# Modulation products of a two-stream transformer: one two-row accumulation, or four 32-column strips of the array

## The chip, the cores and the metric

The kernel runs on one core of a Trainium2 chip (trn2). The metric is device time in microseconds (us) of one execution; a kernel's figure is the median of its runs. A profiled execution leaves a trace of every instruction, with its engine (PE is TensorE's matmuls, PEld its weight loads, DVE VectorE, ACT ScalarE, POOL GpSimd, SP SyncE) and what it waited for.

## The reference

Two residual streams of 256 tokens by 1024 channels (`x` and a context stream) go through two blocks and a last block of another kind, all in float32. Each of the first two blocks normalizes, mixes (a recurrent branch with 16 heads, a convolution branch, a gate), normalizes again and runs a lookup over 16384 experts. Both norms and both residual additions are modulated. The modulation depends on one conditioning vector for each stream:

```python
# silu of the conditioning vector, times a [1024, 6144] matrix, plus a bias
mod = silu(c) @ p['ada_w'] + p['ada_b']
shift1, scale1, gate1, shift2, scale2, gate2 = split(mod, 6)
h = rmsnorm(x, g) * (1 + scale1) + shift1
```

For one layer that is two vectors of 1024 times 48 output tiles of 128 columns; for both layers 96 tiles, whose weights take 512 KB each. Only two columns, one for each stream, are ever multiplied with these weights.

## The kernel before, in words

Channels lie on the 128 partitions, a vector of 1024 as 8 pieces (k tiles), tokens on the free axis (512, both streams side by side). Weights are read as float32 tiles of [128, 8, 128]; `wtile` (L227) loads one on SP's queue, ACT rounds it into `whi` (L238) and DVE writes the rest into `wlo` (L240). `lin` (L251) multiplies with three products for each k tile (`whi` with the high and the low half of the activation, `wlo` with the high half), so a 128 x 512 output (`zps`, `gtps`, `zaps`, `zbps`) takes 24 matmuls at L258.

The **modulation** is made in units of two output tiles by `ada` (L271). Each unit loads two weight tiles `adaw` (SP, L277), multiplies the 8 k tiles of each into two rows of a PSUM tile `adaps` (L279: the stationary operand is `cs`, two columns; the 128 weight columns stream past), copies the two rows to `adarow` (ACT, L281), turns each 2 x 128 piece over with a transpose (L283) and adds the bias into `mod` (DVE, L284). There are 48 units. Eight, with scale 1 and shift 1 of layer 0, stand at the start of the first mixer, ahead of `modnorm` (L326), which forms `ngm` (L335) and then for each k tile `nt` (DVE, L342), `h` (ACT, L344) and the low half of `h` (DVE, L345). 24 are dealt into the mixer of layer 0 and 16 into that of layer 1, the letters 'A' of the table `PLAN` (L33). These share the tag "wraw" with the weights of `wtile`, two buffers, and so also their order on SP's queue.

A **mixer** goes through eight pairs of heads. A pair has a projection and decay part (`ssps` L417, `wps`, `aps` L437, with gate products `gtps`), a score part (`scps` L485, `sc` DVE L489, the turning `btps` L499) and a chain of chunk steps that wait for one another (`bp` L571, `up` L580, `zp` L585, `yp` L557). Other work is put between the parts at places that `PLAN` names; `pop` (L287) starts it, with priorities moved by `BUMP` (L35). What then stands where on each engine is settled by a list scheduler from priorities and estimated durations. So a change in the products changes the order of other work too. ACT reloads its function table (ACT_TABLE_LOAD) where one kind of function follows another.

After the mixer of layer 0 comes its expert lookup, then mixer and lookup of layer 1, then the last block; in the lookups and the last block no unit stands.

`self.blk` (L189) is a constant with two blocks of 64 x 64 ones, the stationary operand of `ssps`.

Of the kernel before, what the change touches and what calls it, by code (L numbers as in the profile page):

```python
# [11 lines left out]
F32 = mybir.dt.float32  # L12
# [4 lines left out]
AF = mybir.ActivationFunctionType  # L17
ALU = mybir.AluOpType
# [4 lines left out]
P = 128  # L23
D = 1024
KO = 8
# [152 lines left out]
class Core:  # L178
# [3 lines left out]
    def consts(self):  # L182
        nc, tc = self.nc, self.tc
        cp = self.cp = self.ctx.enter_context(tc.tile_pool(name="const", bufs=1, reuse_waits="tile"))
        self.ident = cp.tile([P, P], F32, name="ident")
        make_identity(nc, self.ident)
        self.onesd = cp.tile([P, P], F32, name="onesd")
        nc.vector.memset(self.onesd, 1.0 / D)
        self.blk = cp.tile([P, P], F32, name="blk")  # L189
        nc.vector.memset(self.blk, 0.0)  # L190
        nc.vector.memset(self.blk[0:64, 0:64], 1.0)
        nc.vector.memset(self.blk[64:128, 64:128], 1.0)
        self.rmask = cp.tile([P, 2, P], F32, name="rmask")
        nc.scalar.dma_start(self.rmask, self.A["rmask"])
        self.reset = cp.tile([P, 8 * 65], BF16, name="reset")
        nc.vector.memset(self.reset, 1.0)
        nc.vector.memset(self.reset[:, ::65], 0.0)
        self.iota = cp.tile([P, P], F32, name="iota")
        nc.scalar.dma_start(self.iota, self.A["iota"])
        self.cb = {}  # L200
        for n, v in (("neps", NORM_EPS), ("lneps", 4 * LN_EPS), ("gneps", GN_EPS), ("ln512", math.log(512.0)), ("one", 1.0)):
            self.cbias(n, v)
        self.pv = []
        for l in range(2):
            t = cp.tile([P, NPV], F32, name=f"pv{l}")
            nc.scalar.dma_start(t, self.A["pv"][l])
            self.pv.append(t)
        self.pv2 = cp.tile([P, NPV2], F32, name="pv2")
        nc.scalar.dma_start(self.pv2, self.A["pv2"])
        self.mod = [cp.tile([P, 48, 2], F32, name=f"mod{l}") for l in range(2)]  # L210
# [49 lines left out]

    def silu_c(self):
        nc, tc = self.nc, self.tc
        self.cs = self.cp.tile([P, KO, 2], F32, name="cs")
        with tc.tile_pool(name="adap", bufs=1, reuse_waits="tile") as ap:
            c = ap.tile([P, KO, 2], F32, name="cT")
            nc.scalar.dma_start(c, self.A["cT"])
            nc.scalar.activation(self.cs, c, AF.Tanh, scale=0.5)
            nc.vector.tensor_scalar(self.cs, self.cs, 0.5, 0.5, op0=ALU.mult, op1=ALU.add)
            nc.vector.tensor_mul(self.cs, self.cs, c)

    def ada(self, l, m0, n, wpool, wtag, bufs, pp, tag):  # L271

        nc = self.nc
        ps = pp.tile([P, 512], F32, tag=tag, name="adaps")
        for i in range(n):
            w = wpool.tile([P, KO, P], F32, tag=wtag, name="adaw", bufs=bufs)
            nc.sync.dma_start(w, self.A["ada"][l, m0 + i])  # L277
            for k in range(KO):
                nc.tensor.matmul(ps[0:2, i * P:i * P + P], self.cs[:, k, :], w[:, k, :], start=k == 0, stop=k == KO - 1)  # L279
        row = self.wp.tile([2, 2 * P], F32, tag="adarow", name="adarow", bufs=1)  # L280
        nc.scalar.copy(row[:, :n * P], ps[0:2, :n * P])  # L281
        for i in range(n):
            nc.tensor.transpose(ps[:, 2 * i:2 * i + 2], row[:, i * P:i * P + P], self.ident[0:2, 0:2])  # L283
        nc.vector.tensor_tensor(self.mod[l][:, m0:m0 + n, :], ps[:, 0:2 * n].rearrange("p (m c) -> p m c", c=2),  # L284
                                self.par(l, "ada_b", m0, n).unsqueeze(2).to_broadcast([P, n, 2]), op=ALU.add)

    def pop(self, where):  # L287
# [1476 lines left out]
```

## Time and profile before

| | us |
|---|---|
| median of 3 runs (lowest, highest) | 5218.21 (5210.64, 5221.29) |
| profiled execution, by its own time | 5211.48 |
| span of the trace in it | 5209.7 |
| PE busy | 4967.9 (95%) |
| PE weight loads busy | 4170.8 (80%) |
| DVE busy | 3488.0 (67%) |
| ACT busy | 2561.0 (49%) |
| POOL busy | 182.2 (3%) |

Busy times overlap, since the engines run side by side. Matmuls are pipelined, and the end of one is modelled, so that a busy TensorE is not one at its peak. The mean granted clock of TensorE over the span is 0.965 of full speed. "Waits" name the instruction or transfer whose end released the waiting one; the chain is followed back from the last instruction, each time to what released it. A matmul of float32 operands leaves two records in the trace (two passes), so the 768 products of the modulation are 1536 records. Rows show the form of a matmul as stationary rows * columns, then the moving tile.

### The profile page before, as it was taken

Reading aid. Unit: us, or ns where it says so; the run is one execution under the profiler, and the core shown is the slowest. Engines: PE = TensorE matmul, PEld = TensorE weight load, DVE = VectorE, ACT = ScalarE, POOL = GpSimd, SP = SyncE. Lnnn points to the kernel's source line nnn. Section 1 sums busy time; section 2 is a strip of 40 time slices with the busy share of each in tenths; the row PEclk is TensorE's granted clock in tenths of the full one; section 3 lists DMA queues with packets and bytes.
Section 4 is the critical chain, followed back from the end, with each engine's and each line's share of the span. In section 5 each row is a group of like instructions: output and inputs, shape, how many; then the busy total and the mean of one; then the engine's idle time right before and its main releaser. Section 6 shows DMA issues by size and latency. Waiting matters only on the chain.

```text
span 5209.7 us, 86462 instructions
## 1 busy us (share of the span) xinstructions
PE 4967.9 (95%) x33298; PEld 4170.8 (80%) x33298; DVE 3488.0 (67%) x7830; ACT 2561.0 (49%) x4754; POOL 182.2 (3%) x409
## 2 busy tenths in 40 slices
PE   8999998999999999999999999998899999989989
PEld 6677776678777888888887787877889999987888
DVE  4888878558995455555555566656796777765654
ACT  4345444534989322222223445445478544455564
POOL 0000001000000000000000010101000000000000
PEclk9999999999999999999999899888999999999999
DMA  4332323543444644444442332323656877733544
GB/s 137 107 91 88 90 81 93 167 151 101 160 171 163 234 144 142 142 143 142 143 146 70 111 84 78 85 61 92 210 187 222 279 227 238 226 116 118 167 131 146
DMA packets 432974, 740.50 MB, mean 142 GB/s; under 512 B 132210, under 2 KB 273202, under 8 KB 427826
## 3 DMA queue, kind: packets, MB, share of 16 engines
q1 hardware_dynamic: 431042, 732.29, 44.1%
q8 instruction: 262, 4.29, 0.3%
q10 hardware_dynamic: 1520, 2.69, 0.1%
q14 instruction: 150, 1.23, 0.1%
HBM read 622.37 MB, written 112.49 MB: 141 GB/s over the span
## 4 chain that ended last, share of the span: by engine, by line
PE 74%; ACT 12%; DVE 8%; DMA 3%; issue 2%; SPq 0%; ACTq 0%; POOL 0%; DVEq 0%; POOLq 0%
PE v L1180 20%; PE s L258 14%; PE zps L258 5%; ACT ws L1126 3%; PE adaps L279 3%; PE qps L258 2%; PE ops L258 2%; PE gtps L258 2%; ACT pt L1121 2%; PE ops L1368 2%; ACT whi L238 2%; ACT pt L1120 2%; PE bp L571 1%; DVE wlo L240 1%; PE zbps L258 1%
## 5 line engine op out<-in xcount | busy, mean ns | idle before, releaser
L258 PE MATMUL s<-h,whi 128*128 128x512 f32 (+1 forms) x4096 | 1058.7, 343 | 1.3 <-ACT whi L238 0.7
L240 DVE TENSOR_TENSOR wlo<-wraw,whi 128x1024 fp32r<-128x1024 f32 (+2 forms) x602 | 724.7, 1205 | 470.9 <-ACT whi L238 458.4
L238 ACT CAST whi<-wraw 128x1024 fp32r<-128x1024 f32 (+2 forms) x602 | 621.9, 1034 | 727.0 <-PE s L258 200.0
L258 PEld LDWEIGHTS s<-h,whi 128*128 128x128 f32 x4096 | 703.8, 191 | 68.6 <-ACT ge L1136 1.0
L258 PE MATMUL s<-h,wlo 128*128 128x512 f32 (+1 forms) x2048 | 704.2, 344 | 9.1 <-DVE wlo L240 9.1
L1180 PE MATMUL v<-al,vh 128*128 128x512 f32 (+1 forms) x2048 | 689.7, 337 | 0.6 <-DVE al L953 0.6
L1180 PE MATMUL v<-ah,vl 128*128 128x512 f32 (+1 forms) x2048 | 689.2, 337 | 0.0
L1180 PE MATMUL v<-ah,vh 128*128 128x512 f32 (+1 forms) x2048 | 682.7, 338 | 2.1 <-ACT ah L952 1.5
L952 ACT CAST vh<-vraw 128x1024 fp32r<-128x1024 f32 x256 | 261.9, 1050 | 719.2 <-PE v L1180 574.9
L1226 DVE SCALAR_TENSOR_TENSOR x<-v,mod,x 128x256 f32<-128x256 f32 x768 | 333.7, 477 | 272.6 <-PE v L1180 272.1
L1180 PEld LDWEIGHTS v<-ah,vh 128*128 128x128 f32 x2048 | 387.3, 190 | 49.7 <-ACT ah L952 9.4
L1180 PEld LDWEIGHTS v<-al,vh 128*128 128x128 f32 x2048 | 388.8, 190 | 46.3 <-DVE al L953 4.8
L258 PEld LDWEIGHTS s<-h,wlo 128*128 128x128 f32 x2048 | 390.3, 191 | 44.4 <-DVE wlo L240 10.3
L1180 PEld LDWEIGHTS v<-ah,vl 128*128 128x128 f32 x2048 | 388.1, 190 | 40.3 <-issue 1.4
L953 DVE TENSOR_TENSOR vl<-vraw,vh 128x1024 fp32r<-128x1024 f32 x256 | 308.6, 1220 | 98.9 <-ACT vh L952 98.9
L258 PE MATMUL zps<-h,whi 128*128 128x512 f32 (+3 forms) x896 | 293.6, 407 | 15.5 <-DVE lz L363 7.5
L1125 PEld LDWEIGHTS wps<-qt,pt 128*128 128x128 f32 x1536 | 215.8, 190 | 109.5 <-ACT pt L1121 91.2
L1125 PE MATMUL wps<-qt,pt 128*128 128x128 f32 x1536 | 272.3, 292 | 22.2 <-ACT pt L1121 13.6
L1126 ACT COPY ws<-wps 128x512 f32<-128x512 f32 x192 | 210.5, 1097 | 5.7 <-PE wps L1125 5.2
L258 PEld LDWEIGHTS zps<-h,whi 128*128 128x128 f32 (+1 forms) x896 | 167.5, 198 | 52.8 <-issue 16.6
L279 PE MATMUL adaps<-adaw,cs 128*2 128x128 f32 x1536 | 202.0, 274 | 5.4 <-DMA adaw<-ada 3.2
L1121 ACT ACTIVATE pt<-pt,tr,tr 128x128 f32<-128x128 f32 x384 | 180.4, 489 | 2.5
(614 smaller groups left out, 9617.4 us busy)
## 6 DMA issues: line engine op xcount, KB each, us to landing
wraw<-peu SPq DMA_DIRECT2D x256, 512.0 KB, 4.2
vraw<-pev SPq DMA_DIRECT2D x256, 512.0 KB, 4.5
wraw<-win SPq DMA_DIRECT2D x139, 512.0 KB, 3.6
adaw<-ada SPq DMA_DIRECT2D x96, 512.0 KB, 3.6
wd<-ws SPq DMA_DIRECT2D x24, 2048.0 KB, 6.8
wt<-wd SPq DMA_DIRECT2D x32, 1024.0 KB, 6.8
wraw<-w_q SPq DMA_DIRECT2D x32, 512.0 KB, 3.7
gd<-ge SPq DMA_DIRECT2D x64, 256.0 KB, 2.1
```

The source lines that it names most:

```text
L238: nc.scalar.copy(hi, raw)
L240: nc.vector.tensor_sub(lo, raw, hi.bitcast(F32))
L258: nc.tensor.matmul(out, w[wi][:, k, :], a[ai][:, k, ts], start=n == 0, stop=n == 3 * ko - 1)
L279: nc.tensor.matmul(ps[0:2, i * P:i * P + P], self.cs[:, k, :], w[:, k, :], start=k == 0, stop=k == KO - 1)
L952: self.nc.scalar.copy(hi, src)
L953: self.nc.vector.tensor_sub(lo, src, hi.bitcast(F32))
L1120: nc.scalar.activation(pt, self.iota, AF.Abs, bias=tr[3][:, cs])
L1121: nc.scalar.activation(pt, pt, AF.Relu, bias=tr[2][:, cs], scale=tr[4][:, cs])
L1125: nc.tensor.matmul(ps[:, t, :], pt, qt[:, t1 + t], start=True, stop=True)
L1126: nc.scalar.copy(ws[:, :, t0 + t1:t0 + t1 + 4].rearrange("p i t -> p t i"), ps)
L1180: nc.tensor.matmul(ps[:, m, :], va[i][wi][:, ms], aa[i][ai], start=n == 0, stop=n == 3 * GI - 1)
L1226: nc.vector.scalar_tensor_tensor(x[:, k, ts], src[:, m, ts], self.mod[l][:, 40 + k, s:s + 1], x[:, k, ts], op0=ALU.mult, op1=ALU.add)
```

## The change

The eight k tiles of an output tile no longer accumulate in the same two rows. Product k goes to the strip of 32 columns of the array with number k mod 4, and so to the PSUM rows from 32 (k mod 4) on; each strip accumulates two k tiles. The stationary operand must then be 32 columns wide: `csb[:, 2k:2k+32]`, of which the first two are the wanted ones and 30 are others (the next k tiles' columns and the start of the block constant, which now lies in the same tile). ACT copies all 128 rows of the result instead of two. The two transposes become two float32 matmuls by `sum4` [128, 2], whose ones pick rows 0, 32, 64, 96 (and 1, 33, 65, 97): they add the four strips and turn the row over in one, into columns 256 to 259 of the same PSUM tile. `sum4` is built once with one copy and three additions on DVE. From the new `silu_c` on, lines move down: L277 becomes L284, L279 L288, L281 L291, L283 L293, L284 L294, and later ones by ten.

```diff
-        self.blk = cp.tile([P, P], F32, name="blk")
+        self.csb = cp.tile([P, 2 * KO + P], F32, name="csb")
+        self.blk = self.csb[:, 2 * KO:]
...
     def silu_c(self):
-        self.cs = self.cp.tile([P, KO, 2], F32, name="cs")
+        self.sum4 = self.cp.tile([P, 2], F32, name="sum4")
+        nc.vector.tensor_copy(self.sum4, self.ident[:, 0:2])
+        for g in range(1, 4):
+            nc.vector.tensor_add(self.sum4, self.sum4, self.ident[:, 32 * g:32 * g + 2])
...
+            cs = self.csb[:, 0:2 * KO].rearrange("p (k c) -> p k c", c=2)
...
     def ada(self, l, m0, n, wpool, wtag, bufs, pp, tag):
...
             for k in range(KO):
-                nc.tensor.matmul(ps[0:2, i * P:i * P + P], self.cs[:, k, :], w[:, k, :], start=k == 0, stop=k == KO - 1)
-        row = self.wp.tile([2, 2 * P], F32, tag="adarow", name="adarow", bufs=1)
-        nc.scalar.copy(row[:, :n * P], ps[0:2, :n * P])
+                gs = slice(32 * (k % 4), 32 * (k % 4) + 32)
+                nc.tensor.matmul(ps[gs, i * P:i * P + P], self.csb[:, 2 * k:2 * k + 32], w[:, k, :], start=k < 4 and i == 0,
+                                 stop=k >= 4, skip_group_check=True)
+        row = self.wp.tile([P, 2 * P], F32, tag="adarow", name="adarow", bufs=1)
+        nc.scalar.copy(row[:, :n * P], ps[:, :n * P])
         for i in range(n):
-            nc.tensor.transpose(ps[:, 2 * i:2 * i + 2], row[:, i * P:i * P + P], self.ident[0:2, 0:2])
-        nc.vector.tensor_tensor(self.mod[l][:, m0:m0 + n, :], ps[:, 0:2 * n].rearrange("p (m c) -> p m c", c=2),
+            nc.tensor.matmul(ps[:, 256 + 2 * i:258 + 2 * i], row[:, i * P:i * P + P], self.sum4, start=True, stop=True)
+        nc.vector.tensor_tensor(self.mod[l][:, m0:m0 + n, :], ps[:, 256:256 + 2 * n].rearrange("p (m c) -> p m c", c=2),
```

The number of matmuls and transfers is the same; DVE gets four instructions more, ACT six table loads more (all in pairs of layer 1). The scheduler's order changes in both mixers; that of the lookups and of the last block does not. On TensorE the 768 products stand in 197 uninterrupted stretches before and in 109 after. Dealt four to a round, the 109 stretches make 231 rounds; without any interruption it would be 192.

On **DVE at the start of the first mixer**, from the first bias addition on, before:

```order
L284 TENSOR_TENSOR mod_92<-adaps,pv_86 128x4
L240 TENSOR_TENSOR wlo<-wraw,whi 128x1024
L284 TENSOR_TENSOR mod_92<-adaps,pv_86 128x4
L240 TENSOR_TENSOR wlo<-wraw,whi 128x1024
L284 TENSOR_TENSOR mod_92<-adaps,pv_86 128x4 x6
L335 SCALAR_TENSOR_TENSOR ngm<-mod_92,pv_86 128x16
L342 SCALAR_TENSOR_TENSOR nt<-x,ngm,nr 128x256 x3
L345 SCALAR_TENSOR_TENSOR h_120<-nt,mod_92,h_119 128x256 x3
```

The same place in the changed kernel (the rows left out are three more groups of L352 and L355, three instructions each):

```order
L269 TENSOR_TENSOR sum_99<-sum_99,ident 128x2 x3
L294 TENSOR_TENSOR mod_92<-adaps,pv_86 128x4 x8
L345 SCALAR_TENSOR_TENSOR ngm<-mod_92,pv_86 128x16
L352 SCALAR_TENSOR_TENSOR nt<-x,ngm,nr 128x256 x4
L355 SCALAR_TENSOR_TENSOR h_124<-nt,mod_92,h_123 128x256 x4
L352 SCALAR_TENSOR_TENSOR nt<-x,ngm,nr 128x256 x3
L355 SCALAR_TENSOR_TENSOR h_124<-nt,mod_92,h_123 128x256 x3
...
L242 TENSOR_TENSOR wlo<-wraw,whi 128x1024
```

The two `wlo` that stood between the first units now come after the whole of `modnorm`. On SP's queue the 16 `adaw` loads of the start stand in one row ahead of the first `wraw`, where two `wraw` stood among them; on TensorE four products of `zps` stand ahead of the first that reads `wlo`, and 44 behind it.

On **TensorE in the score part of the fourth pair of layer 0**, before:

```order
L279 MATMUL adaps<-adaw,cs 2x128 x10
L485 MATMUL scps<-kr,be 128x2x64 x8
L279 MATMUL adaps<-adaw,cs 2x128
L485 MATMUL scps<-kr,be 128x2x64 x4
L279 MATMUL adaps<-adaw,cs 2x128 x2
L485 MATMUL scps<-kr,be 128x2x64 x8
L279 MATMUL adaps<-adaw,cs 2x128 x3
L499 MATMUL btps<-ident,be 128x128 x4
L283 MATMUL adaps<-ident,adarow 128x2 x2
L279 MATMUL adaps<-adaw,cs 2x128
```

The same place after:

```order
L288 MATMUL adaps<-adaw,csb 32x128 x16
L293 MATMUL adaps<-sum_99,adarow 128x2 x2
L495 MATMUL scps<-kr,be 128x2x64 x8
L288 MATMUL adaps<-adaw,csb 32x128
L495 MATMUL scps<-kr,be 128x2x64 x4
L288 MATMUL adaps<-adaw,csb 32x128 x5
L495 MATMUL scps<-kr,be 128x2x64 x8
L288 MATMUL adaps<-adaw,csb 32x128 x10
L509 MATMUL btps<-ident,be 128x128 x4
L293 MATMUL adaps<-sum_99,adarow 128x2 x2
```

Two whole units now stand in the score part, where one was spread over it and the chain. Behind it, the first chain steps of this pair hold no product of the modulation (before, one in each step), the third unit comes in stretches of 3, 2, 2, 2 and 7 in later steps, and products of `zbps` and `zaps` that stood behind the chain fill its last steps. In layer 1, 22 `gtps` products move ahead of the score part of a pair, and its first three or four chain steps hold no other product.

## Rows read from the trace of the kernel before

**Rows 1.** The page: busy times of the engines, then the chain by line.
```profile
PE 4967.9 (95%) x33298; PEld 4170.8 (80%) x33298; DVE 3488.0 (67%) x7830; ACT 2561.0 (49%) x4754; POOL 182.2 (3%) x409
...
PE v L1180 20%; PE s L258 14%; PE zps L258 5%; ACT ws L1126 3%; PE adaps L279 3%; PE qps L258 2%; PE ops L258 2%; PE gtps L258 2%; ACT pt L1121 2%; PE ops L1368 2%; ACT whi L238 2%; ACT pt L1120 2%; PE bp L571 1%; DVE wlo L240 1%; PE zbps L258 1%
```

**Rows 2.** Modulation tile by line: count, min/median/max ns, first and last start, form.
```profile
L279 PE MATMUL adaps<-adaw,cs x1536: 269/272/422, 16.8 to 3650.5; 128*2 128x128 f32 x192
...
L281 ACT COPY adarow<-adaps x48: 344/361/362, 20.5 to 3651.5; 2x256 f32<-2x256 f32 x48
```

**Rows 3.** Timeline, first units and one product alone: start, length, engine, work.
```profile
21.29 3.36 PEld L279 LDWEIGHTS adaps<-adaw,cs 128*2 128x2 f32 x32
21.29 3.66 PE L279 MATMUL adaps<-adaw,cs 128*2 128x128 f32 x32
...
440.18 0.38 PE L279 MATMUL adaps<-adaw,cs 128*2 128x128 f32 x2
440.49 0.49 PE L571 MATMUL bp<-uv,sc 128*128 128x128 f32 x2
```

**Rows 4.** Timeline of TensorE in the last block: one strip, then several, same shapes.
```profile
4878.13 0.33 PE L1610 MATMUL lyp<-qi,lS 128*64 128x64 f32 x2
4878.39 0.32 PE L1616 MATMUL lzp<-lvt,lktt 64*32 64x64 f32 x8
...
4908.10 0.65 PE L1657 MATMUL aop<-pT,fvt 128*64 128x256 f32 x2
...
4908.99 0.65 PE L1657 MATMUL aop<-pT,fvt 128*64 128x256 f32 x4
```

**Rows 5.** Window of first loads: from:to, length; PE, PEld, DVE, ACT, POOL busy; clock, DMA, GB/s.
```profile
8.00:16.00 8.00, 8.00 (x15) 2.99 (x14) 0.76 (x7) 5.46 (x9) 0.00 (x0) 1.00 0.98 362
```

**Rows 6.** Timeline of DVE at the first norm.
```profile
22.88 1.23 DVE L240 TENSOR_TENSOR wlo<-wraw,whi 128x1024 fp32r<-128x1024 f32 x1 [1.25 <-ACT whi L238]
...
51.74 0.16 DVE L284 TENSOR_TENSOR mod<-adaps,pv 128x4 f32<-128x4 f32 x1 [3.56 <-PE adaps L283]
...
52.15 1.28 DVE L342 SCALAR_TENSOR_TENSOR nt<-x,ngm,nr 128x256 f32<-128x256 f32 x3
...
53.34 1.27 DVE L345 SCALAR_TENSOR_TENSOR h<-nt,mod,h 128x256 fp32r<-128x256 f32 x3
```

**Rows 7.** Chain of waits from the first unit to the first projection: start, length, what.
```profile
21.15 0.21 PE adaps L283 x2
...
53.63 13.39 PE zps L258 x45
```

**Rows 8.** Windows, modulation products alone: from:to, length; PE, PEld busy; clock, DMA share, GB/s.
```profile
52.00:200.00 148.00, 11.29 (x96) 7.76 (x96) 0.93 0.30 88
200.00:800.00 600.00, 85.39 (x576) 37.31 (x576) 0.99 0.30 89
800.00:2960.00 2160.00, 23.95 (x192) 15.14 (x192) 0.98 0.44 144
2960.00:3640.00 680.00, 46.78 (x384) 30.12 (x384) 0.88 0.28 79
```

**Rows 9.** Windows of pair parts, all work; columns as in rows 5.
```profile
420.38:430.76 10.38, 10.11 (x89) 7.79 (x89) 9.70 (x21) 2.80 (x6) 0.00 (x0) 1.00 0.35 95
430.76:458.50 27.74, 27.74 (x200) 21.54 (x198) 19.23 (x89) 10.68 (x39) 3.98 (x13) 1.00 0.27 79
458.50:506.62 48.12, 46.58 (x320) 34.42 (x319) 40.42 (x85) 25.23 (x42) 3.71 (x7) 1.00 0.37 105
2970.84:2992.76 21.92, 21.30 (x181) 16.85 (x179) 17.56 (x40) 11.63 (x24) 0.22 (x2) 0.98 0.41 122
3514.60:3538.48 23.88, 19.10 (x123) 16.23 (x121) 20.09 (x43) 11.06 (x23) 0.12 (x1) 0.71 0.09 17
3538.48:3559.80 21.32, 15.89 (x94) 12.13 (x93) 17.75 (x77) 9.83 (x36) 7.19 (x15) 1.00 0.39 108
```

**Rows 10.** Table loads of ACT by line: count, busy, mean ns.
```profile
L420 ACT ACT_TABLE_LOAD x11 | 14.1, 1283 | 0.2
```

More of the change, by code (lines that the diff above doesn't have):

```diff
@@ L266, in silu_c @@
             nc.scalar.dma_start(c, self.A["cT"])
-            nc.scalar.activation(self.cs, c, AF.Tanh, scale=0.5)
-            nc.vector.tensor_scalar(self.cs, self.cs, 0.5, 0.5, op0=ALU.mult, op1=ALU.add)
-            nc.vector.tensor_mul(self.cs, self.cs, c)
+            cs = self.csb[:, 0:2 * KO].rearrange("p (k c) -> p k c", c=2)
+            nc.scalar.activation(cs, c, AF.Tanh, scale=0.5)
+            nc.vector.tensor_scalar(cs, cs, 0.5, 0.5, op0=ALU.mult, op1=ALU.add)
+            nc.vector.tensor_mul(cs, cs, c)
     def ada(self, l, m0, n, wpool, wtag, bufs, pp, tag):
```

## The prediction, made from the rows above

> **What bounds the kernel now.** I read the page first: TensorE is busy 95% of the span, DVE 67%, ACT 49%, and the chain of waits gives the modulation products (L279) 3% of its time [rows 1]. So the engine that the change unloads is the one that mostly sets the end. Then the products themselves, by tile: 1536 records, 272 ns long each in the median [rows 2]. Their length says little of what each costs, because they overlap; the timeline of the first units has 32 of them in 3.66 us [rows 3], and (3.66 - 0.27) / 31 = 0.109 us is what each adds. One unit is thus 3.5 us of TensorE and two transposes, 0.21 us on the chain [rows 7]. A product that stands alone takes 0.31 us until the next work begins (440.18 to 440.49) against 2 x 0.109 = 0.22 in a row [rows 3], so that each interruption costs about 0.09 us. Next the windows with the products alone: of their busy time 85 us lie in layer 0's pairs (200 to 800), 47 in layer 1's (2960 to 3640), 11 and 24 in the places between [rows 8], and nearly all of the rest ahead of the first norm. Last the windows of whole pair parts [rows 9], which tell what else is full where the products stand. In layer 0's score part DVE is busy 9.70 of 10.38 us, in the chain part behind it TensorE 27.74 of 27.74, and behind that TensorE 46.58 of 48.12. So there TensorE is the limit over a pair, but not in each part.
>
> **The change, part by part.**
>
> *The products.* Before: 1536 x 0.109 = 167 us, and 197 stretches x 0.09 = 18, together 185 us of TensorE. After: 231 rounds of two passes. What a round takes, no row shows for four strips of full height and 128 columns. Two rows come near it. In the last block eight records in four strips of 32 columns, each over 64 rows, take 0.32 us, where two records in one strip of 64 columns take 0.33; and four records in two strips, each over all 128 rows, take 0.65 us, as two records in one strip do [rows 4]. In both cases the strips beside the first are free. If that holds, 231 x 2 x 0.109 = 50 us and 109 stretches x 0.09 = 10, together 60. The other end is no overlap at all: 167 + 10. I take the first, the rows being nearer to it on both sides (number of strips, height), and give a little back below.
>
> *The 32 columns* of each weight load instead of two: the same eight records in 0.32 us load 32 columns each [rows 4], so nothing is charged.
>
> *The sums.* Each unit gets two float32 matmuls of two passes in place of two transposes of one record: two records more, at 0.11 us, 48 times: 10 us of TensorE. The lower end is the pace of the transposes, 0.21 / 2 [rows 7], the upper twice that: 10 to 20 us.
>
> So TensorE loses 185 - 70 = 115 us of work at most. I take **105**, a share of 0.57 of what the products cost now; the ends are 115 and about 0. The 10 between are for rounds whose weights come late.
>
> A rule speaks against this. The rows: in the 3.66 us of the 32 products, 32 weight loads lie beside them, busy 3.36 us, each on all 128 rows, and the products still follow every 0.109 us [rows 3], so a load on the same rows is hidden here. The Trainium skill ("TensorE: Matmul & The Clock Gate", section "Part 3: Packing small matmuls — row/col tiling") says that a weight load overlaps with matmuls in flight only when the row group differs. Here all four strips use all row groups, so by that rule the four loads of every round would be exposed. It is the third rival below.
>
> *The copy of the row* (ACT): 361 ns at 2 x 256 [rows 2]; with 128 rows the columns are as many, so I charge nothing. The nearest row with 128 x 256 is DVE's 1.28 / 3 = 0.43 us [rows 6]; then 48 x 0.07 = 3 us, on an engine busy 49%. The four instructions for `sum4` and the copy of `csb` stand ahead of the first unit, where DVE is busy 0.76 of 8 us [rows 5]. No transfer is added; the loads are issued earlier, since a buffer is freed earlier.
>
> *The start.* Now `mod` is complete at 51.74 + 0.16 [rows 6], because a unit takes TensorE 3.8 us. After, a unit takes 8 passes at 0.109, the sums 0.4 and two interruptions, about 1.5, less than its two loads: 1.05 MB at 362 GB/s [rows 5] is 2.9 us. So the loads set it: 16 x 0.524 MB and about 1 MB of the input, at 362 from 8 us on, end near 34, and `mod` is there at about 35. But the gain is not 17. The first `wlo` now stands on DVE behind the whole norm: 16 `nt` and 16 low halves at 0.43 [rows 6] are 13.6 us, to 49; `wlo` takes 1.23 [rows 6], to 50; then 44 products of `zps` are left, at 13.39 / 45 = 0.30 us as now [rows 7] 13 us, to 63. They can be quicker, since the 13.39 us hold waits for the norm; half of it is my other end, to 57. Before, they ended at 53.63 + 13.39 = 67.0 [rows 7]. I take a gain of **5** (4 to 10).
>
> *Between the mixers' pairs* (52 to 200, 800 to 2960): 35 us [rows 8], of which 0.57 is 20. Here a unit's tiles come through two buffers and its load is waited for, so I let half reach the end: **10** (0 to 20).
>
> *Layer 0, six pairs*: 85 us, 0.57 is 49, or 8 for each pair. In the score part DVE has 0.7 us free [rows 9], so there little can go. What helps is that the score part takes two whole units, the chain's slots come free, and `zbps` and `zaps` move into its last steps, out of the part where TensorE is 97% busy. Chain steps with no other work wait for one another: in layer 1's last pair TensorE is busy 15.89 of 21.32 us there [rows 9]. So the first, bare steps give only part. I take 5 of the 8 for each pair: **30** (6 to 49).
>
> *Layer 1, six pairs*: 47 us, 0.57 is 27, or 4.4 each. But the last pair, whose score part holds no product at all, is no quicker in it: 23.88 us against 21.92 with products, with DVE busy 20.09 and a mean granted clock of 0.71, so some of it at the lower of the two levels, 1.2 GHz, where TensorE had less to do [rows 9]. I take 2 for each pair, 12, less the six new table loads at 1.283 us [rows 10], 8: **4** (-20 to 27).
>
> Sum: 5 + 10 + 30 + 4 = 49 us. The profiled execution took 5211.5 by its own time (span 5209.7), so 5162.5; it lies 6.7 below the median, and from the median it is 5169. I take 5167, near the latter.
>
> **The rivals.**
>
> 1. *Freed, but not on the path.* In the score parts DVE ends last, in the chain the steps' own waits, at the start the loads. For it: DVE's 93% [rows 9]; against: TensorE's 97 to 100% in the other parts. Then the start gives 5, the places between 5, a pair of layer 0 1.5, layer 1 nothing: 19 us, 5199 by the median; within 10 to 30 of gain.
>
> 2. *All of it reaches the end*, by work that moves up into every gap: 105 us, 5113. For it: the 95% [rows 1]. Against: the parts named.
>
> 3. *Loads not hidden.* A load takes 3.36 / 32 = 0.105 us [rows 3]. If each of the 462 passes had to wait for its loads, the four going side by side, that is 49 us less cut, 56 left. At the same share (49 of 105) it gives 26 us: 5192. The rule named above would do this; the rows of L279 and L1616 speak against it [rows 3, 4].
>
> 4. *The strips don't run side by side.* Four full-height strips might take turns. Then 88 fewer stretches save 8 us, the sums cost 10, and only the order changes: 5218, no change.
>
> 5. *Slower: cover lost in the twelve pair windows.* With the products shorter, TensorE has less to do while DVE works in the score part, and its granted clock falls, as in layer 1's last pair (0.71 against 0.98, 2.0 us longer) [rows 9]. If all twelve windows pay 2.0 and gain nothing: 24, and 8 for the table loads, less 15 from the start and the places between: 17 us slower, 5235. It decides from a loss of (15 - 8) / 12 = 0.6 us a window. Against it: two units still stand in the score part.
>
> **How the numbers follow.** A measurement of this kernel can tell about 0.2% (10 us) from no change. Chances: the forecast (35 to 75 us) 0.45, rival 1 0.20, rival 2 0.12, rival 3 0.07, rival 4 0.06, rival 5 0.10. Faster: 0.45 + 0.12 + 0.07 and four fifths of rival 1, 0.80; the same: the rest of rival 1 and rival 4, 0.10; slower 0.10. The range runs from rival 2's 5113, rounded to 5112, to 5212, past rival 1's slower end of 5208; it leaves out rivals 4 and 5.
>
> **What would show it.** Right: L288's records bunch, eight in about 0.22 us plus the tail; the products' busy time by windows falls below 100 us; the first `zps` chain ends near 61; layer 0's pairs take some 5 us less each, layer 1's 1 or less. Wrong: rounds of 0.22 us or more for each pass (rivals 3, 4); score parts as long as before with the chain no shorter (rival 1); a granted clock under 0.9 in the score parts of layer 0 (rival 5).

## The result, and the profile after

The changed kernel is a little slower: 5249.84 us in the median of 7 runs (5238.67 to 5262.66) against 5218.21, a ratio of 1.0067 (95% interval 1.0051 to 1.0082). The ratios in this text are estimates from all runs, not quotients of the medians. 5167 was forecast, with 5212 as the upper end. The profiled execution took 5260.9 us by its own time (span 5258.9), 11 above its median; the one before 5211.5 (span 5209.7).

The page of the changed kernel, answering to [rows 1]: busy times, the chain by engine, the chain by line.

```profile
PE 4948.1 (94%) x33394; PEld 4181.1 (80%) x33394; DVE 3486.4 (66%) x7834; ACT 2567.3 (49%) x4760; POOL 191.6 (4%) x409
...
PE 71%; ACT 12%; DVE 11%; DMA 3%; issue 2%; POOL 0%; ACTq 0%; SPq 0%; DVEq 0%; POOLq 0%
PE v L1190 20%; PE s L260 14%; PE zps L260 4%; ACT ws L1136 3%; PE ops L260 2%; PE qps L260 2%; ACT pt L1131 2%; PE gtps L260 2%; PE scps L495 2%; DVE wlo L242 2%; PE ops L1378 2%; ACT whi L240 2%; ACT pt L1130 2%; PE bp L581 1%; PE yp L567 1%
```

The products are no longer among the fifteen lines that the chain names (L279 had 3% there), and TensorE is busy 20 us less. But the span is 49 us longer, so it waits 69 us more. The medians differ by 32 us only: the execution profiled after lies 11 above its median, the one before 7 below. So the 49 us that are placed below hold some 18 that belong to these two executions and not to the change.

**The products did what the forecast said.** The timeline of the first units, answering to [rows 3] (start, length, engine, work):

```profile
24.50 1.07 PE L288 MATMUL adaps<-adaw,csb 128*32 128x128 f32 x30
...
25.68 0.37 ACT L291 COPY adarow<-adaps 128x256 f32<-128x256 f32 x1 [1.78 <-PE adaps L288]
...
26.11 0.61 PE L293 MATMUL adaps<-sum,adarow 128*128 128x2 f32 x4 [0.54 <-ACT adarow L291]
...
26.64 0.64 PE L288 MATMUL adaps<-adaw,csb 128*32 128x128 f32 x16
```

30 records, eight passes of up to four strips, take 1.07 us, and 16 take 0.64; before, 32 took 3.66. With the tail of 0.27 that the forecast took off, that is (1.07 - 0.27) / 7 = 0.114 us for a pass of all the strips. The copy takes 0.37 us as before, the sums 0.61 where the transposes took 0.28 in the same view (24.88 us). The windows with the products alone, answering to [rows 8] (from:to, length, PE and PEld busy, clock, DMA share, GB/s):

```profile
52.00:200.00 148.00, 6.26 (x116) 3.84 (x116) 0.91 0.34 101
200.00:850.00 650.00, 41.42 (x556) 21.42 (x556) 0.91 0.30 85
850.00:2960.00 2110.00, 9.58 (x192) 5.79 (x192) 0.98 0.45 146
2960.00:3680.00 720.00, 21.80 (x384) 12.07 (x384) 0.83 0.26 75
```

Busy time of the products outside the start: 167.4 us before, 79.1 now, although the granted clock of TensorE (the column behind PEld) is lower in three of the four rows.

**Where the time came from.** The starts of the pairs' first matmuls (`ssps`) cut the span into stretches. To the second pair's start: 182.0 us against 192.5, so 10.5 less. The next six pairs of layer 0: 28.8 more. From there to the second pair of layer 1: 13.2 less. Its next six pairs: 32.8 more. The rest, in which one unit stands: 11.3 more. That is 49 together. The rest, from the start of the last pair on, is code that no edit touches but for that unit; over the profiled executions of all nine kernels here it took 1704.8 to 1722.0 us, so its 11 us are no finding. The loss is in the pairs, 61.6 us in twelve.

Windows of the last four of the six pairs of layer 0, and of the six of layer 1 (from:to, length; PE, PEld, DVE, ACT, POOL busy; clock, DMA, GB/s). Before:

```profile
399.44:827.67 428.23, 420.80 (x2777) 312.13 (x2776) 347.71 (x897) 207.20 (x432) 38.24 (x92) 0.98 0.30 88
2964.62:3503.12 538.50, 522.07 (x5307) 435.29 (x5306) 352.66 (x983) 264.08 (x611) 58.12 (x138) 0.89 0.28 79
```

After:

```profile
398.80:845.92 447.12, 418.81 (x2800) 323.84 (x2797) 340.18 (x895) 204.51 (x430) 47.04 (x92) 0.90 0.29 83
2969.71:3541.01 571.30, 534.25 (x5328) 443.28 (x5328) 356.71 (x983) 271.88 (x616) 58.93 (x138) 0.84 0.26 75
```

These rows can be read as a sum. Length less PE busy is TensorE's idle time. A matmul at the lower level (1.2 GHz) takes about twice as long (32 records of L288 take 1.94 us at 532.84 in the changed kernel, at half clock, and 1.08 at 529.52 in the run `csum_late` below, at full clock), so of the busy time (1 - clock) x length is what the clock adds; the rest is work at full clock. (The clock is rounded to 0.01, which is 1 us in a pair, and idle time at the lower level is counted in it too, by at most 0.8 us; differences under 1 us say nothing.) For one pair of layer 0, length = work + idle + clock: before 107.1 = 103.1 + 1.9 + 2.1, after 111.8 = 93.5 + 7.1 + 11.2. For one of layer 1: 89.8 = 77.1 + 2.7 + 9.9, and 95.2 = 73.8 + 6.2 + 15.2. The work fell by 9.6 and 3.3 us (8 and 4.4 were forecast). Idle time and clock took back more than that.

**Where in a pair.** The score part (`scps`, L495) and the turning behind it, in the pair that starts at 504.6 before and 511.1 after. Before:

```profile
521.10:532.90 11.80, 11.80 (x103) 9.25 (x103) 11.37 (x24) 3.60 (x7) 0.12 (x1) 1.00 0.23 77
532.90:536.90 4.00, 3.73 (x31) 2.95 (x30) 2.91 (x9) 2.22 (x6) 0.29 (x1) 1.00 0.34 57
```

After:

```profile
524.80:545.50 20.70, 18.04 (x129) 14.86 (x132) 13.26 (x26) 4.17 (x8) 1.40 (x4) 0.60 0.25 78
545.50:552.10 6.60, 6.60 (x46) 6.14 (x46) 2.11 (x8) 2.26 (x6) 0.29 (x1) 0.50 0.61 159
```

11.8 us became 20.7 and 4.0 became 6.6, with DVE busy 2 us longer in the first and less in the second: TensorE runs at half clock. Ahead of it stands this chain of waits (start, length, what):

```profile
521.70 4.04 POOL csum L905
...
525.83 1.24 DVE pre L459
...
527.66 0.70 DVE pre L464
...
529.26 2.07 PE scps L495 x8
```

and this wait in TensorE's timeline:

```profile
527.78 0.46 PE L581 MATMUL bp<-uv,sc 128*128 128x128 f32 x2 [1.81 <-DVE zb L604]
```

POOL's running sum `csum` takes 4.0 us here. Behind it on POOL stands the clearing of 128x8 elements of `pre`, on which DVE's scan waits, and TensorE then stands idle for 1.8 us. After it the clock is at the lower level: eight records of `scps` take 2.07 us. In the kernel before they took 1.16, by its timeline:

```profile
523.11 1.16 PE L485 MATMUL scps<-kr,be 64*128 64x128 f32 x8
```

At the end of these pairs stands a wait as long, which is new too:

```profile
502.06 0.71 PE L260 MATMUL gtps<-h,whi 128*128 128x512 f32 x2 [2.15 <-ACT v L368]
```

Behind it come gate products one after another, and the clock stays up; in the five such places from 389 to 837 us it fell once, for 3.4 us. So a wait of 2 us doesn't lower the clock everywhere. What stands behind the wait may decide; no run tested it.

So two theories. **A**: the new order lets TensorE idle, and that lowers the clock. **B**: the strips themselves leave TensorE too little to do, whatever the order.

### The profile page after: what moved, and what is told of

It is laid out like the page before. It is cut to its first block, busy times and chain, and to the rows that moved or that the text cites. A ratio compares the mean times of both kernels' runs of the same rounds, so it can differ in the third digit from the quotient of the medians.

```text
span 5258.9 us, 86601 instructions
## 1 busy us (share of the span) xinstructions
PE 4948.1 (94%) x33394; PEld 4181.1 (80%) x33394; DVE 3486.4 (66%) x7834; ACT 2567.3 (49%) x4760; POOL 191.6 (4%) x409
## 4 chain that ended last, share of the span: by engine, by line
PE 71%; ACT 12%; DVE 11%; DMA 3%; issue 2%; POOL 0%; ACTq 0%; SPq 0%; DVEq 0%; POOLq 0%
PE v L1190 20%; PE s L260 14%; PE zps L260 4%; ACT ws L1136 3%; PE ops L260 2%; PE qps L260 2%; ACT pt L1131 2%; PE gtps L260 2%; PE scps L495 2%; DVE wlo L242 2%; PE ops L1378 2%; ACT whi L240 2%; ACT pt L1130 2%; PE bp L581 1%; PE yp L567 1%
## 5 line engine op out<-in xcount | busy, mean ns | idle before, releaser
L1135 PE MATMUL wps<-qt,pt 128*128 128x128 f32 x1536 | 272.7, 292 | 22.4 <-ACT pt L1131 13.2
L260 PE MATMUL zps<-h,wlo 128*128 128x512 f32 (+3 forms) x448 | 182.1, 407 | 13.6 <-DVE wlo L242 13.5
```

Source lines behind the costliest of these rows:

```text
L260: nc.tensor.matmul(out, w[wi][:, k, :], a[ai][:, k, ts], start=n == 0, stop=n == 3 * ko - 1)
L1135: nc.tensor.matmul(ps[:, t, :], pt, qt[:, t1 + t], start=True, stop=True)
```

## Experiments

### Order and products apart

Both halves of the change can be had alone. The kernel's instructions are issued as before, then each engine is held to an order read from the other kernel's program (edges of order without a wait; `ORDER` is that order, `per` the engine's instructions as issued):

```diff
         build(tc, args)
+        impose(tc, nc)
...
+def impose(tc, nc):
...
+    for e, t in ORDER.items():
+        seq = np.cumsum(np.frombuffer(zlib.decompress(base64.b85decode(t)), "<i4"))
...
+        for a, b in zip(seq, seq[1:]):
+            tc.add_manual_dep(per[e][b], per[e][a].name, info, reason="order")
```

Strips in the old order:

> The changed kernel (four strips, the sums by matmul), but every engine issues its instructions in the order of the kernel before. Theory A, the order: the new order leaves TensorE idle for some 1.8 us ahead of the score part of a pair, the granted clock falls to 0.5 there, and score part and turning take twice as long. Then this kernel has the old clock (low for about 20 us between 200 and 830, not 117) and gets the shorter products: 5150 to 5195 us, score parts of 10 to 12 us. Theory B, the strips themselves: four strips in a fourth of the time leave TensorE too little to do while DVE works, in whatever order. Then the score parts run at 0.5 here too, and the time is 5230 to 5265 us.

Measured: 5209.18 us (10 runs) against 5210.84, ratio 1.0001 (0.9984 to 1.0018). Neither range holds it. In its trace the second pair starts 8.7 us sooner than before (183.8 against 192.5), and the first two pairs lose as much again. The windows of the same pairs as above, layer 0 and layer 1:

```profile
399.41:821.04 421.63, 407.62 (x2802) 307.71 (x2801) 346.82 (x897) 207.38 (x432) 35.91 (x92) 0.98 0.30 89
2958.85:3489.17 530.32, 501.86 (x5332) 428.17 (x5331) 352.45 (x983) 265.95 (x611) 59.34 (x138) 0.88 0.28 81
```

Two-row products in the new order:

> The kernel before (products into two rows, transposes), but every engine issues its instructions in the order of the changed kernel. Theory A, the order: the idle 1.8 us ahead of the score part come with the order, the clock falls as in the changed kernel, and the products take longer on top: 5260 to 5340 us. Theory B, the strips: with the long products TensorE keeps its clock through the score parts, and the time is that of the kernel before, 5205 to 5235 us.

Measured: 5304.17 us (4 runs), ratio 1.0173 (1.0145 to 1.0201), in A's range. Its windows:

```profile
422.08:872.51 450.43, 424.54 (x2776) 319.96 (x2773) 340.53 (x895) 203.95 (x430) 47.10 (x92) 0.95 0.28 83
3018.52:3587.71 569.19, 538.49 (x5304) 442.67 (x5304) 356.90 (x983) 271.92 (x616) 58.71 (x138) 0.88 0.26 75
```

The new order costs 93 us with the old products, and 0.66% (1.0067 against 1.0001), some 34 us, with the strips. The strips give back 54 us in it (5304 to 5250), yet in the old order they gain nothing. By the sum, in us for one pair of layer 0 (the four of the window) and of layer 1:

| | length | work | idle | clock | layer 1: length | work | idle | clock |
|---|---|---|---|---|---|---|---|---|
| before | 107.1 | 103.1 | 1.9 | 2.1 | 89.8 | 77.1 | 2.7 | 9.9 |
| strips, old order | 105.4 | 99.8 | 3.5 | 2.1 | 88.4 | 73.0 | 4.7 | 10.6 |
| rows, new order | 112.6 | 100.5 | 6.5 | 5.6 | 94.9 | 78.4 | 5.1 | 11.4 |
| after (strips, new order) | 111.8 | 93.5 | 7.1 | 11.2 | 95.2 | 73.8 | 6.2 | 15.2 |

In layer 0 the idle time comes mostly with the order (1.9 to 6.5); in layer 1 either half alone brings 2.0 to 2.4 us. In layer 0 the clock falls with both: it costs 3.5 us more by the order alone, 9.1 by the two together. So A holds for a part of the order's loss, and B is half right: the strips make the clock fall much further where the order has made TensorE wait. In the first two pairs strips lower it in the old order too: 107.8 us each there at a clock of 0.94, against 103.5 at 1.00 before.

### The wait ahead of the score part

POOL's `csum` behind the clearing of `pre`, in the new order; one number in POOL's table moves in each of seven pairs:

```diff
 POOL, one pair:
-csum<-csum,cc   pre   krp<-kr   pre
+pre   krp<-kr   pre   csum<-csum,cc
```

> The changed kernel in its own order, but POOL's running sum of squares (csum, 4.0 us there) stands behind the small clearing of the next scan (pre) instead of ahead of it, in seven pairs of layer 0; nothing else moves. Theory A, a wait starts the low clock: without the csum ahead of it the scan on DVE comes some 1.8 us sooner, TensorE does not wait ahead of bp, and the granted clock stays up through the score part: low clock between 200 and 830 under 60 us instead of 116, pairs 3 to 6 shorter by 5 to 10 us each, total 5205 to 5225. Theory B, the strips themselves leave too little to do: the wait goes, the clock falls all the same (over 95 us low), total 5235 to 5255.

Measured: 5241.53 us (5 runs), ratio 1.0057 (1.0033 to 1.0081). The time lies in B's range and is not clear of the changed kernel's 1.0067. Between 200 and 830 us the lower clock lasted 79 us, between A's 60 and B's 95. One row for the four pairs of layer 0:

```profile
402.00:834.09 432.09, 405.37 (x2801) 311.88 (x2798) 344.10 (x895) 204.02 (x430) 36.49 (x92) 0.94 0.29 86
```

A pair takes 108.0 us instead of 111.8 (A said 5 to 10 less), work 94.9, idle 6.7, clock 6.5. So by these two traces the wait cost 4.7 of the clock's 11.2 us. But TensorE's timeline a little later in the same part shows what is late next (the end of the row tells the wait):

```profile
526.05 0.46 PE L581 MATMUL bp<-uv,sc 128*128 128x128 f32 x2 [0.50 <-DVE zb L604]
...
531.29 0.61 PE L293 MATMUL adaps<-sum,adarow 128*128 128x2 f32 x4 [0.69 <-ACT adarow L291]
532.94 0.82 PE L495 MATMUL scps<-kr,be 64*128 64x128 f32 x5 [1.04 <-DVE sc L499]
```

`bp` (L581) now waits 0.50 us. Then the sums wait 0.69 us for ACT's copy, the next `scps` 1.04 us for DVE, and the clock falls there, some 6 us later than before. In the last pair the later `csum` is itself waited for, by the sums of a norm:

```profile
849.45 2.08 PE L830 MATMUL lnm<-csum,onesd 128*128 128x512 f32 x2 [6.20 <-POOL csum L905]
```

In the changed kernel TensorE waited 1.54 us at that place. So the edit took one wait away and made another, outside the four pairs, and the total can't tell A from B.

The same wait filled instead of taken away, in four pairs (the lines that place the added products in the order are left out):

```diff
             for wi, ai in ((0, 0), (0, 1), (1, 0)):
+                if fill and n == 22:
+                    for q in range(FILL):
+                        z = nc.tensor.matmul(out, w[0][:, q % ko, :], self.zz[:, 0:1].to_broadcast([P, 512]), start=False, stop=False)
...
```

> The changed kernel in its own order, with eight added products by zeros (128x128 by 128x512, into an open sum, so that they change nothing) on TensorE at the place of the 1.8 us wait ahead of bp, in pairs 3 to 6 of layer 0; the wait itself stays on DVE. Theory A, TensorE's idling there is what lowers the clock: pairs 3 to 6 shorter by 5 to 10 us each though work was added, total 5210 to 5235. Theory B, the light score part lowers it: pairs 3 to 6 as long as before or 0.2 longer, total 5240 to 5265.

Measured: 5242.55 us (10 runs), ratio 1.0062 (1.0045 to 1.0080). The time again lies in B's range and is not clear of the changed kernel's.

```profile
401.50:838.09 436.59, 413.29 (x2833) 319.14 (x2830) 339.91 (x895) 204.13 (x430) 46.98 (x92) 0.94 0.29 85
```

A pair takes 109.2 us, 2.7 less, although 1.8 us of work were added to each and the order is the same. B said as long or longer, A 5 to 10 less. The sign is A's and the size is not, since the clock falls at the next waits here too, for 13.7 us in each of the four pairs (unfilled, 13.7 to 27.3). The trace of the changed kernel was 11 us above its median, so 2.7 a pair may be too much.

### All waits of the pairs filled

In both orders, products whose result is not read stand at waits of 0.33 us or more in the pairs, about as many as fit:

```diff
+    def fill(self, ps, done):
+        for n, at, c in FILL.get(self.nu, ()):
+            if n == done:
+                for q in range(c):
+                    z = self.nc.tensor.matmul(ps[:, 384:512], self.onesd, self.ident, start=False, stop=False, skip_group_check=True)
...
```

> The kernel with strips in the old order, with 144 added products of 128x128 by 128x128 (0.22 us each, their results are not read) on TensorE at the places in the pairs where it waited 0.33 us or more, about as many as fit in each wait. Theory A, the low clock that the waits bring is what costs: low clock between 200 and 830 falls from 51 us to under 20, each of pairs 1 and 2 gets 4 to 6 us shorter, pairs 3 to 6 some 2 to 3, layer 1's pairs 2 to 4, total 5165 to 5195. Theory C, DVE and ACT set the pace there and the clock costs nothing: the pairs keep their lengths, total 5200 to 5225.

Measured: 5194.52 us (8 runs) against 5208.92, ratio 0.9970 (0.9957 to 0.9983): at the upper end of A's range, and faster than the kernel before and than the strips alone (1.0001; 0.9984 to 1.0018), with 144 x 0.22 = 32 us of useless work more. The first two pairs, then the four, then layer 1:

```profile
185.37:392.19 206.82, 199.11 (x1418) 150.93 (x1416) 171.69 (x447) 102.28 (x216) 18.14 (x46) 1.00 0.30 89
392.19:813.83 421.64, 412.69 (x2863) 313.06 (x2862) 346.88 (x897) 207.15 (x432) 35.91 (x92) 0.98 0.31 89
2954.68:3487.20 532.52, 518.74 (x5521) 440.72 (x5520) 351.74 (x983) 264.22 (x611) 59.52 (x138) 0.90 0.29 80
```

The first two pairs take 103.4 us instead of 107.8, at full clock: A's 4 to 6. The four take 105.4 as with the strips alone, and layer 1's 88.8 instead of 88.4: there A failed, since idle time only turned into added work. So 9 us of the gain have a place; the rest cannot be placed by these traces.

> The changed kernel in its own order with POOL's csum behind pre, and with 89 added products of the same kind at the waits of 0.33 us or more in the pairs. Theory A, the low clock is what still costs there: low clock between 200 and 830 falls from 89 us to under 35, pairs 1 to 6 some 4 to 6 us shorter, total 5195 to 5220. Theory C, DVE and ACT set the pace: pairs as long as with csum behind pre alone, total 5232 to 5255.

Measured: 5227.67 us (8 runs), ratio 1.0033 (1.0013 to 1.0054), between the ranges. Its profiled execution is the slowest of its runs (5211.94 to 5253.70), and the four pairs in it,

```profile
398.25:828.76 430.51, 408.21 (x2864) 309.83 (x2862) 343.76 (x895) 204.52 (x430) 35.95 (x92) 0.95 0.30 86
```

take 107.6 us each, against 108.0 with `csum` moved alone. By its time it is some 0.3% faster than the changed kernel (1.0033 against 1.0067), with 89 products more, but where that comes from this trace doesn't show.

### What such a cut gains in the old order

Seven of the eight products of a tile keep two of their 128 columns, so the modulation lacks seven k tiles in the other columns, and only the time counts. The order is held to that of the kernel before:

```diff
-                nc.tensor.matmul(ps[0:2, i * P:i * P + P], self.cs[:, k, :], w[:, k, :], start=k == 0, stop=k == KO - 1)
+                c = P if k == 0 else 2
+                nc.tensor.matmul(ps[0:2, i * P:i * P + c], self.cs[:, k, :], w[:, k, 0:c], start=k == 0, stop=k == KO - 1)
```

> The kernel before in its own order, with seven of the eight products of each modulation tile cut to two of their 128 columns: the modulation then lacks seven k tiles in all other columns, but every instruction, wait and transfer stays. Some 125 of TensorE's 200 us for the products go, in the old order, without a strip or a sum. Theory D, the pairs' ends are set by DVE and ACT, and TensorE work that goes turns into waits and low clock there: pairs 3 to 6 within 3 us of before, total 5185 to 5225. Theory E, the old order is bound by TensorE and the strips in it gained nothing because its short stretches fill few rounds: with the products nearly out, pairs 3 to 6 are 5 to 8 us shorter each, total 5110 to 5165.

Measured: 5200.34 us (10 runs) against 5215.12, ratio 0.9969 (0.9956 to 0.9982), theory D. First the products alone in layer 0's six pairs:

```profile
189.00:807.00 618.00, 41.43 (x576) 21.97 (x576) 0.95 0.29 90
```

Then the four pairs of layer 0 and the six of layer 1, all work:

```profile
389.29:807.15 417.86, 400.62 (x2777) 309.41 (x2776) 345.66 (x897) 206.86 (x432) 35.91 (x92) 0.96 0.29 90
2945.09:3487.22 542.13, 518.05 (x5307) 442.80 (x5306) 352.93 (x983) 265.62 (x611) 58.83 (x138) 0.83 0.27 79
```

A pair of layer 0: 104.5 = 96.0 + 4.3 + 4.2. Work fell by 7.1 us, the pair by 2.6. Of layer 1: 90.4 = 71.0 + 4.0 + 15.4; work fell by 6.1, and the pair is 0.6 longer, for clock and idle time take all of it back. The thinned products are not gone: they are busy 41.4 us there, about as the strips are in their new order (41.4 for 556 records, part of it at the lower clock), where it was 85.4 before [rows 8]. So the cut that was forecast, with no order changed, gains 15 us and not 49. Whether a deeper cut, or one with the waits filled, gains more was not tried.

## Why the prediction was wrong

- *The products* (115 us less work at most, 105 taken): right in mechanism and about in size. A pass of four strips takes 0.114 us, and the products' busy time fell below 100, as the forecast's sign asked. Work fell by 9.6 us in a pair of layer 0 (8 forecast) and 3.3 in one of layer 1 (4.4).
- *Loads not hidden* (rival 3): no. Weight loads of 32 columns on all rows are hidden in those 0.114 us (by TensorE's rows at 24.50, where 30 records take 1.07 us, loads and all). The rule of the Trainium skill ("TensorE: Matmul & The Clock Gate", "Part 3: Packing small matmuls — row/col tiling"), that a load overlaps only with matmuls of another row group, does not hold for strips of columns in this trace.
- *The start* (5 us, 4 to 10): 8 us by the first `ssps` (82.3 against 90.4 us), but that it lies in the range is luck. `mod` came at 39.8, not 35: the clock was 0.53 from 30.3 to 40, so that the last two units took 3.4 us each, and each unit's sums waited some 0.5 us for ACT's copy. The first 48 records of `zps` ended at 66.1, not near 61, and at 67.7 before: 1.6 us of gain by the path that was forecast. The other 6 come mostly from a wait that the sum doesn't name and that is gone after:

```profile
71.46 1.19 PE L258 MATMUL zps<-h,whi 128*128 128x512 f32 x2 [3.78 <-DVE lz L363]
```

- *Between the pairs* (10): about 16, of which 13 from the last pair of layer 0 to the second of layer 1 (with code that no edit touches) and 2 in the first pair.
- *Layer 0, six pairs* (30 us gained, 6 to 49): 28.8 lost. This is the step that failed: it took "TensorE 27.74 of 27.74" and "46.58 of 48.12" [rows 9] for the sign that TensorE is the limit over a pair, let 5 of 8 us through, and counted the new order there as a help. The thinned products show that 7.1 us of work less make a pair 2.6 shorter in the unchanged order, and the new order costs a pair 5.5 us with the old products (107.1 to 112.6). TensorE was full because the order had filled it; the products were the filler of the score part, where DVE's 9.70 of 10.38 us [rows 9] said so.
- *Layer 1* (4 gained, -20 to 27): 32.8 lost. The last pair without products, 23.88 us at a clock of 0.71 [rows 9], was read, and weighed too little.
- *The new order* was charged only its table loads and the first norm's `wlo`. It costs 93 us with the old products and some 34 with the strips. That `csum` stands ahead of `pre` on POOL could have been read from the order; POOL's queue was not weighed.
- *Rival 5* named what happened, the clock in the pair windows, at a chance of 0.10 and 2.0 us a window, and its sign came (0.60 in the score part above). The loss was 5.1 a window; the clock alone added 9.1 us to a pair of layer 0 and 5.3 to one of layer 1. Its cause, less work beside DVE, is only a part: in the last four of layer 0's six pairs the strips alone added nothing to the clock's share (2.1 to 2.1), with the order's waits they did.

What stays open: in layer 1 the order costs 5 us a pair (89.8 to 94.9), of which the table loads can be 1.3. In the changed kernel's trace every second of these pairs takes 97 to 99 us and the others 92, and only in the long ones does TensorE wait 1.5 us at `wps` for ACT's `ld` (L444), which stands behind a table load. Whether that is the cause was not tried, nor was the wait of 2.15 us at the end of layer 0's pairs taken away. And the clock's part rests on one trace of each kernel.

## What to carry to other kernels

A busy share says that an engine is full, not that it is the limit. Before speeding up work that fills gaps, thin it out (same instructions, fewer columns) in the unchanged order: one run tells what a cut of that size gains there. Where a scheduler sets the order, run the new operation in the old order and the old operation in the new one; the two together rarely tell which of them cost the time.

## What the runs showed of the hardware

An addition of 128x512 on POOL and an operation of DVE on 128x512 held one another up where they met. All seven of `csum` with this form, before and after (after the bar: busy us, mean ns, idle before):

```profile
L895 POOL TENSOR_TENSOR csum<-csum,cc 128x512 f32<-128x512 f32 x7 | 11.1, 1585 | 189.8 <-DVE cc L888 163.8 <-ACT th L439 26.0
```

```profile
L905 POOL TENSOR_TENSOR csum<-csum,cc 128x512 f32<-128x512 f32 x7 | 24.4, 3482 | 157.9 <-ACT uv L592 107.4 <-DVE cc L898 50.5
```

With DVE idle beside it, it took 1.27 us (at 880.92 of `rows_new_order`). The one at 521.70 took 4.04: DVE ran five 128x512 operations in a row from before its start to 524.60, and it ended 1.14 us behind them. In `csum_late` it was DVE's operation that took longer, 1.79 us where the next took 0.68:

```profile
419.33 1.27 POOL L905 TENSOR_TENSOR csum<-csum,cc 128x512 f32<-128x512 f32 x1
419.35 1.79 DVE L475 TENSOR_TENSOR kr<-r,ee 128x512 f32<-128x512 f32 x1
421.07 0.68 DVE L478 TENSOR_TENSOR kd<-kd,k 128x512 f32<-128x512 f32 x1
```

After a wait of 1.81 us TensorE went on at 1.2 GHz through the score part and the turning, though it was busy 18.04 of 20.70 and 6.60 of 6.60 us there. After a wait of 2.15 us, with gate products behind it, it went on at 2.4 GHz in four of five places. Work that nobody reads, put into the waits of the pairs, made two pairs 4.4 us shorter each.

Four strips of 32 columns and all 128 rows ran in the time of one: 0.114 us for a pass, against 0.109 for a pass of a single product before.
